# A decoder trunk on one core: round trips on SyncE's queue, polyphase matrices fetched a chunk ahead, products half a chunk later, the norm's sums added on GpSimd

## The chip, the cores and the metric

The kernel runs on one core of a Trainium2 chip. A core has five engines with queues of their own: TensorE (PE in the profile; PEld is its weight load), VectorE (DVE), ScalarE (ACT), GpSimd (POOL) and SyncE (SP), which here only issues transfers. Each engine works through its instructions in order and waits at its head for what the next one needs. The metric is the device time of one execution in microseconds.

## The reference

Two layers act on x of 512 tokens and 1024 features. Layer 0 has a causal Conformer convolution module, layer 1 differential attention; each is followed by a SwiGLU network and a gated per-layer embedding. The change lies in the convolution module:

```python
u = rms_norm(h, conv_norm_g[j])
a = x @ w_pw1 + b_pw1                                # here x is u
u = a[..., :D_MODEL] * jax.nn.sigmoid(a[..., D_MODEL:])
u = lax.conv_general_dilated(u, dw_w[:, None, :], window_strides=(1,),
    padding=[(CONV_WIDTH - 1, 0)], feature_group_count=D_MODEL) + dw_b   # 31 taps per feature
u = jax.nn.silu(layer_norm(u, ln_g, ln_b))           # mean and variance over 1024 features
return u @ w_pw2 + b_pw2
```

## The kernel before

Features lie on the 128 partitions, in 8 chunks of 128, and the 512 tokens along the free axis. Every product of the large matrices is made three times, with the operands split into a high and a low part (`mm3`). A weight tile comes from memory to `wraw` (2 buffers, SyncE's queue), ACT casts its high part to `whi`, DVE or GpSimd subtracts it to `wlo` (4 buffers each): `weight`, L137 to L150.

The convolution stage takes the chunks c = 0 to 7 in turn (loop at L407). Each has two halves of 24 matmuls, first for the gate, then for the value (`half`, L279). DVE and ACT form the gated product. The 31 taps of a chunk are then done one of two ways while the next chunk's halves run:

- Chunks 0, 1, 3, 5 and 7: some taps on TensorE with diagonal matrices (`pe_taps`: 4 for chunk 1, 14 for chunk 7), some on ACT and GpSimd (ACT multiplies, GpSimd adds, through four buffers `C2`/`C3`), the rest on DVE (`other_taps`).
- Chunks 2, 4 and 6 (`PHASED`): the product goes to memory and comes back with the tokens dealt to partitions by their remainder modulo 4 (`phased_in`: one store `pi`, four loads `C<-pi`). 36 products with 128 x 128 matrices do all taps (`phased_taps`). The result goes to memory and back the same way (`phased_out`: ACT copies it out of PSUM, store `po`, four loads `B<-po`, then one DVE operation).

Before the change, `phased_in` and `phased_out` issue their transfers on ACT's queue. The polyphase matrices come as twelve tiles a chunk with three matrices each, through six slots `D`, each issued just ahead of its three products.

The layer norm needs two sums over all features, of y and of its square. `moments` (L385) makes them on TensorE: for each chunk a product with a matrix of ones into `sums["mean"]` (L404; for chunks 1 to 7) and one into `sums["sq"]` (L405), fp32, 512 wide. After chunk 7, DVE takes the statistics (L454 to L459), a row is spread by L228, and y is shifted (L466 on DVE, L468 on GpSimd), scaled (L489), goes through SiLU (L490), is split (L492, L494) and enters the next matrix product. Products of the embedding's features (`project`) stand in TensorE's order there as fill.

The order on each engine is set by a scheduler that simulates the program; `tc.issue_after(x)` keeps what stands inside behind the instruction x. So the order of the source is only a wish.

Of the kernel before, what the change touches and what calls it, by code (L numbers as in the profile page):

```python
# [15 lines left out]
ALU = mybir.AluOpType  # L16
# [68 lines left out]
def trunk(ctx, tc, xT, pT, wts, diag, dww, vec, rel, onehot, lamv, out):  # L85
# [48 lines left out]

    wnext = [0]

    def weight(n=1024, pieces=1, between=(), eng=V):  # L137
        i = wnext[0]
        wnext[0] += 1
        raw = sb([P, 1024], "wraw", 2)  # L140
        hi = sb([P, 1024], "whi", 4, F32R)
        lo = sb([P, 1024], "wlo", 4, F32R)
        for k in range(pieces):
            cut = slice(k * n // pieces, (k + 1) * n // pieces)
            nc.sync.dma_start(raw[:, cut], wts[i, :, cut])
            if k < len(between):
                between[k]()
            A.copy(hi[:, cut], raw[:, cut])  # L148
            eng.tensor_tensor(lo[:, cut], raw[:, cut], f(hi[:, cut]), ALU.subtract)  # L149
        return hi, lo  # L150
# [86 lines left out]
    norm.chunk(0)  # L237
    w1 = weight(pieces=2, between=(load(1), load(2)))
    pairs = [(w1, w0)]
    for c in range(3, NC):  # L240
# [44 lines left out]
    def wt(c, j):  # L285
        return dwt[:, c * KW + j : c * KW + j + 1]

    def pe_taps(c):

# [5 lines left out]
        for j in range(PE_TAPS[c]):  # L295
            if j % 4 == 0:
                n = min(4, PE_TAPS[c] - j)
                dg = sb([P, 4, P], f"D{TAPS.index((c, j)) % 6}", 1)
                nc.sync.dma_start(dg[:, :n], diag[TAPS.index((c, j)), :, :n])
            last_tap[0] = T.matmul(  # L300
# [7 lines left out]
    def phased_in(c, src):  # L308

        d = dram.tile([P, S], F32, tag=f"pi{c}", name=f"pi{c}")  # L310
        nc.scalar.dma_start(d, src)
        xs = ups[c] = sb([P, NPH, LEAD + P], f"C{c // 2 % 2}", 2)
        G.memset(xs[:, :, :LEAD], 0.0)
        for i in range(NPH):
            nc.scalar.dma_start(
                xs[i * FG : (i + 1) * FG, :, LEAD:],
                bass.AP(d.tensor, d.offset + i * P, [[S, FG], [FG * S, NPH], [1, P]]),
            )

    def phased_taps(c, acc):  # L320
        for g in range(NPH):
            for m0 in range(0, LAGS, 3):
                i = TAPS.index((c, g, m0))
                dg = sb([P, 4, P], f"D{i % 6}", 1)
                nc.sync.dma_start(dg[:, :3], diag[i, :, :3])
                for m in range(m0, min(m0 + 3, LAGS)):
                    last_tap[0] = T.matmul(
                        acc[:, g * P : (g + 1) * P], dg[:, m - m0], ups[c][:, g, LEAD - m : LEAD - m + P],
                        start=(m == 0), stop=(m == LAGS - 1),
                    )  # L330

    def phased_out(c):
# [3 lines left out]
        d = dram.tile([P, S], F32, tag=f"po{c}", name=f"po{c}")  # L336
        nc.scalar.dma_start(d, o)
        both_ = sb([P, 2, S], f"B{c}", 1)
        for g in range(NPH):
            nc.scalar.dma_start(  # L340
                both_[g * FG : (g + 1) * FG, 1].rearrange("p (r n) -> p r n", r=NPH),
# [9 lines left out]
    def other_taps(c):  # L351
# [6 lines left out]
        for j in range(a, b):  # L358
            if j == a:
                A.activation(pacc, tap(j), AF.Identity, scale=wt(c, j), bias=col("dw_b", c))  # L360
            else:
                pr = sb([P, S], f"C{2 + j % 2}", 2)
                A.activation(pr, tap(j), AF.Copy, scale=wt(c, j))
                G.tensor_tensor(pacc, pacc, pr, ALU.add)
        yc = sb([P, S], f"B{c}", 1)
        alone = c in ALONE
# [14 lines left out]
    shrow = sb([P, S], "shrow", 1)  # L381
    sums = {}
    last_moment = [None]

    def moments(c):  # L385
# [8 lines left out]
        if c < SHIFT - 1:  # L394
            return
        for i in range(SHIFT) if c == SHIFT - 1 else (c,):
            if i == 0:
                sums["sq"] = tp()
            if i == 1:
                sums["mean"] = tp()  # L400
            sq = wk()
            A.activation(sq, y[i], AF.Square)
            if i > 0:
                T.matmul(sums["mean"], ones, y[i], start=(i == 1), stop=(i == NC - 1))  # L404
            last_moment[0] = T.matmul(sums["sq"], ones, sq, start=(i == 0), stop=(i == NC - 1))  # L405

    for c in range(NC):  # L407
# [6 lines left out]
        if c + 1 < NC:  # L414
            pairs.append((weight(), weight())[::-1])
        if c > 0:
# [28 lines left out]
    with tc.issue_after(last_tap[0].ins):  # L445
        moments(NC - 3)
        moments(NC - 2)
    moments(NC - 1)

# [453 lines left out]
def _layout(a):  # L903
# [44 lines left out]
    for i, (c, *at) in enumerate(TAPS):  # L948
        if c not in PHASED:
            for k in range(min(4, PE_TAPS[c] - at[0])):  # L950
                diag[i, np.arange(P), k, np.arange(P)] = dw[at[0] + k, c]
            continue
        g, m0 = at
        for m in range(m0, min(m0 + 3, LAGS)):
            for a_ in range(NPH):
                for b_ in range(NPH):
                    lag = NPH * m + b_ - a_
                    if 0 <= lag < KW:
                        diag[i, a_ * FG + f, m - m0, b_ * FG + f] = dw[KW - 1 - lag, c, g * FG + f]

# [40 lines left out]
```

## Time and profile before

| what | before |
|---|---|
| median of 3 runs | 1321.56 us (1321.38 to 1324.51) |
| profiled execution, whole time | 1322.03 us |
| its span, first to last instruction | 1320.2 us |
| matmuls on TensorE | 5852, mean clock 0.989 |
| convolution stage | 0 to about 192 us of the span |
| idle of TensorE in windows 0 to 26, 26 to 101, 101 to 192 us | 5.5, 0.6, 13.4 us |

In a timeline row stand the start in us, the time, engine and line, what is written from what, and in brackets the idle time before it and what ended it. One fp32 product is two rows on PE. A row of a group has its count behind x, then the busy time and the mean in ns, then idle time and its cause. A wait row has the sum in us, the count, and the longest. SPq and ACTq are the transfers that an engine's queue issues.

### The profile page before, as it was taken

How to read it: one execution, taken by the hardware profiler on the slowest of the kernel's cores; microseconds unless marked ns; L12 is line 12 of the kernel's file. 1: busy time of each engine (PE TensorE's matmuls, PEld its weight loads, DVE VectorE, ACT ScalarE, POOL GpSimd, SP SyncE). 2: the span in 40 equal slices, each digit the busy share in tenths (PEclk: the TensorE clock that was granted, in tenths of full speed). 3: DMA queues.
4: the chain of work that ended last, by engine and by line, in shares of the span. 5: the costliest groups of instructions: out<-in, count | busy, mean ns of one | idle time of the engine just before them, and what ended most of it. 6: DMA issues, size and time to landing. Idle time of an engine off the chain costs nothing. (4 is left out here: it accounts for less than half of the span.)

```text
span 1320.2 us, 15336 instructions
## 1 busy us (share of the span) xinstructions
PE 1283.0 (97%) x5852; PEld 1049.5 (79%) x5852; DVE 755.1 (57%) x1168; ACT 526.1 (40%) x830; POOL 258.4 (20%) x208
## 2 busy tenths in 40 slices
PE   8999889999999999999999998899999999999998
PEld 6777658888888888888888887778888888888887
DVE  6988684644344434455668887946543344334445
ACT  5644253422122222244466676734322222222342
POOL 5844342100000000022254544222000000000030
PEclk8999889999999999999999999999999999999999
DMA  6354412232322222233212321313223233332231
GB/s 218 110 170 155 132 33 94 82 97 98 104 98 98 97 96 96 80 104 102 87 65 83 102 73 41 103 34 126 96 96 96 96 97 99 102 97 93 76 123 65
DMA packets 45830, 129.21 MB, mean 98 GB/s; under 512 B 5267, under 2 KB 13587, under 8 KB 45756
## 3 DMA queue, kind: packets, MB, share of 16 engines
q1 hardware_dynamic: 39888, 122.70, 27.9%
q10 hardware_dynamic: 5868, 5.53, 1.3%
q8 instruction: 46, 0.75, 0.2%
q14 instruction: 28, 0.23, 0.1%
HBM read 124.52 MB, written 3.69 MB: 97 GB/s over the span
## 5 line engine op out<-in xcount | busy, mean ns | idle before, releaser
L148 ACT CAST whi<-wraw 128x1024 fp32r<-128x1024 f32 (+2 forms) x214 | 218.6, 1026 | 587.9 <-PE mm L156 367.8
L154 PE MATMUL mm<-A,wlo 128*128 128x512 f32 (+1 forms) x1096 | 426.0, 392 | 7.9 <-ACT A L492 3.8
L155 PE MATMUL mm<-A,whi 128*128 128x512 f32 (+1 forms) x1096 | 429.5, 393 | 1.4 <-DVE A L494 0.9
L156 PE MATMUL mm<-A,whi 128*128 128x512 f32 (+1 forms) x1096 | 426.9, 390 | 0.0
L149 DVE TENSOR_TENSOR wlo<-wraw,whi 128x1024 fp32r<-128x1024 f32 (+2 forms) x207 | 255.4, 1237 | 64.0 <-ACT whi L148 63.7
L154 PEld LDWEIGHTS mm<-A,wlo 128*128 128x128 f32 x1096 | 206.9, 189 | 54.7 <-ACT A L492 4.6
L155 PEld LDWEIGHTS mm<-A,whi 128*128 128x128 f32 x1096 | 207.0, 189 | 47.6 <-DVE A L169 3.2
L156 PEld LDWEIGHTS mm<-A,whi 128*128 128x128 f32 x1096 | 207.1, 189 | 43.5 <-issue 1.4
L188 POOL TENSOR_TENSOR acc<-acc,wk 128x512 f32<-128x512 f32 x42 | 68.6, 1632 | 781.8 <-issue 671.2
L155 PE MATMUL mm<-B,whi 128*128 128x512 f32 x352 | 136.9, 389 | 0.0
L156 PE MATMUL mm<-B,whi 128*128 128x512 f32 x352 | 136.9, 389 | 0.0
L154 PE MATMUL mm<-B,wlo 128*128 128x512 f32 x352 | 136.3, 389 | 0.0
L542 DVE TENSOR_TENSOR big<-mm,rb 128x512 f32<-128x512 f32 x44 | 30.4, 691 | 126.2 <-PE mm L156 126.2
L550 DVE TENSOR_TENSOR h<-mm,h 128x512 f32<-128x512 f32 x48 | 33.0, 691 | 120.7 <-PE mm L156 120.7
L540 DVE TENSOR_TENSOR big<-mm,rb 128x512 f32<-128x512 f32 x44 | 30.4, 691 | 99.3 <-PE mm L156 92.9
L154 PEld LDWEIGHTS mm<-B,wlo 128*128 128x128 f32 x352 | 66.1, 188 | 13.8
L156 PEld LDWEIGHTS mm<-B,whi 128*128 128x128 f32 x352 | 66.1, 188 | 13.7
L155 PEld LDWEIGHTS mm<-B,whi 128*128 128x128 f32 x352 | 66.1, 188 | 13.6
L156 PE MATMUL mm<-whi,A 128*128 128x512 f32 x192 | 75.7, 395 | 0.0
L155 PE MATMUL mm<-wlo,A 128*128 128x512 f32 x192 | 75.0, 396 | 0.0
L154 PE MATMUL mm<-whi,A 128*128 128x512 f32 x192 | 74.8, 396 | 0.0
L213 POOL TENSOR_TENSOR r<-v,mhalf 128x8 f32<-128x8 f32 (+1 forms) x31 | 47.5, 1532 | 121.7 <-DVE v L211 99.2
(193 smaller groups left out, 1426.1 us busy)
## 6 DMA issues: line engine op xcount, KB each, us to landing
wraw<-in_wts SPq DMA_DIRECT2D x194, 512.0 KB, 3.5
D<-in_diag SPq DMA_DIRECT2D x36, 192.0 KB, 3.9
wraw<-in_wts SPq DMA_DIRECT2D x16, 384.0 KB, 2.9
h<-in_xT SPq DMA_DIRECT2D x8, 256.0 KB, 5.3
bias<-scr ACTq DMA_DIRECT2D x8, 256.0 KB, 3.2
out_t<-h SPq DMA_DIRECT2D x7, 256.0 KB, 2.0
wraw<-in_wts SPq DMA_DIRECT2D x4, 256.0 KB, 3.4
wraw<-in_pT SPq DMA_DIRECT2D x4, 256.0 KB, 3.3
```

The source lines that it names most:

```text
L148: A.copy(hi[:, cut], raw[:, cut])
L149: eng.tensor_tensor(lo[:, cut], raw[:, cut], f(hi[:, cut]), ALU.subtract)
L154: T.matmul(acc, al, bh, start=first, stop=False)
L155: T.matmul(acc, ah, bl, start=False, stop=False)
L156: return T.matmul(acc, ah, bh, start=False, stop=last)
L188: self.eng.tensor_tensor(self.acc, self.acc, sq, ALU.add)
L213: last_pow[0] = G.tensor_tensor(r[:, :n], v[:, :n], mhalf[:, :n], ALU.pow)
L540: V.tensor_tensor(tg, pg, rb, ALU.mult)
L542: V.tensor_tensor(tu, pu, rb, ALU.mult)
L550: V.tensor_tensor(h[m], acc, h[m], ALU.add)
```

## The change

It has these parts, all in the convolution stage. The transfers of `phased_in` and `phased_out` are issued by SyncE, not ACT. The polyphase matrices come in tiles of four, nine tiles a chunk: for each of the four groups lags 0 to 3 and 4 to 7, and one tile with lag 8 of all groups; groups 2 and 3 use the `C5` buffers besides the `D` slots. All of a chunk's tiles are requested together, behind the weights of the chunk before (`after_weights`, with `pair_loads`). In the loop, the products of a phased chunk are written behind the next chunk's second half, not between its halves. The sums of the layer norm: the squares of chunks 1 to 6 are added on GpSimd to `sums["acc"]`, which starts as chunk 0's square, the values of chunks 1 to 6 to `macc`, and TensorE makes two products for each sum at the end. `issue_after(last_tap)` around `moments` is gone. An activation that calls for SiLU's table stands in chunk 7, ahead of its use.

```diff
-        TAPS += [(_c, g, m) for g in range(NPH) for m in range(0, LAGS, 3)]
+        TAPS += [(_c, g, m) for g in range(NPH) for m in (0, 4)] + [(_c, None, LAGS - 1)]
...
-            nc.sync.dma_start(raw[:, cut], wts[i, :, cut])
+            loaded[0] = nc.sync.dma_start(raw[:, cut], wts[i, :, cut])
...
+    def after_weights(c):
+        return tc.issue_after(pair_loads[c].ins)
...
     def phased_in(c, src):
-        nc.scalar.dma_start(d, src)
+        nc.sync.dma_start(d, src)
...
-            nc.scalar.dma_start(
+            nc.sync.dma_start(
                 xs[i * FG : (i + 1) * FG, :, LEAD:],
...
+    def phased_mats(c):
+        i = TAPS.index((c, 0, 0))
+        mats, k = [], 0
+        for g in range(NPH):
+            if g < 2:
+                two = []
+                for m in range(2):
+                    two.append(sb([P, 4, P], f"D{(i + k) % 6}", 1))
+                    nc.sync.dma_start(two[m], diag[i + 2 * g + m])
+                    k += 1
+            else:
+                both_ = sb([P, 2, 4, P], "C5", 2)
+                two = both_[:, 0], both_[:, 1]
+                for m in range(2):
+                    nc.sync.dma_start(two[m], diag[i + 2 * g + m])
+            mats.append(two)
+            if g == 0:
+                last = sb([P, 4, P], f"D{(i + k) % 6}", 1)
+                nc.sync.dma_start(last, diag[i + 2 * NPH])
+                k += 1
+        return mats, last
...
     def phased_taps(c, acc):
+        with after_weights(c):
+            mats, last = phased_mats(c)
         for g in range(NPH):
-            for m0 in range(0, LAGS, 3):
-                i = TAPS.index((c, g, m0))
-                dg = sb([P, 4, P], f"D{i % 6}", 1)
-                nc.sync.dma_start(dg[:, :3], diag[i, :, :3])
...
+            for m in range(LAGS):
+                w = last[:, g] if m == LAGS - 1 else mats[g][m // 4][:, m % 4]
...
         A.copy(o, accs[c])
-        nc.scalar.dma_start(d, o)
+        nc.sync.dma_start(d, o)
...
             if i == 0:
-                sums["sq"] = tp()
-            if i == 1:
-                sums["mean"] = tp()
+                A.activation(sums["acc"], y[0], AF.Square)
+                continue
             sq = wk()
             A.activation(sq, y[i], AF.Square)
-            if i > 0:
-                T.matmul(sums["mean"], ones, y[i], start=(i == 1), stop=(i == NC - 1))
-            last_moment[0] = T.matmul(sums["sq"], ones, sq, start=(i == 0), stop=(i == NC - 1))
+            if i < NC - 1:
+                G.tensor_tensor(sums["acc"], sums["acc"], sq, ALU.add)
+                if i > 1:
+                    G.tensor_tensor(macc, y[1] if i == 2 else macc, y[i], ALU.add)
+                continue
+            for n, part, one in (("mean", macc, y[i]), ("sq", sums["acc"], sq)):
+                T.matmul(sums[n], ones, part, start=True, stop=False)
+                last_moment[0] = T.matmul(sums[n], ones, one, start=False, stop=True)
...
             pg = half(wg)
-            pe_taps(c - 1)
+            if c - 1 not in PHASED:
+                pe_taps(c - 1)
             pa = half(wa)
+            if c - 1 in PHASED:
+                pe_taps(c - 1)
...
+        if c == NC - 1:
+            A.activation(sb([P, 8], "lam", 1), vt[:, :8], AF.Silu)
...
-            with tc.issue_after(last_tap[0].ins):
-                moments(c - 3)
+            moments(c - 3)
```

What the scheduler makes of it is seen at three places. The first is TensorE around chunk 6's products. Before, `mm_1129` takes chunk 6's products (L327, input `C_214`, matrices `D_230` and on), `mm_1104` is chunk 7's first half and `mm_1190` its second:

```order
L156 MATMUL mm_1104<-A_43_170,whi_967 128x512
L327 MATMUL mm_1129<-C_214_1040,D_230_1130 128x128 x3
L327 MATMUL mm_1129<-C_214_1040,D_231_1135 128x128 x3
L327 MATMUL mm_1129<-C_214_1040,D_232_1140 128x128 x3
L327 MATMUL mm_1129<-C_214_1040,D_233_1145 128x128 x3
L327 MATMUL mm_1129<-C_214_1040,D_234_1150 128x128 x3
L327 MATMUL mm_1129<-C_214_1040,D_235_1155 128x128 x3
L327 MATMUL mm_1129<-C_214_1040,D_236_1160 128x128 x3
L154 MATMUL mm_1190<-A_19_105,wlo_974 128x512
L327 MATMUL mm_1129<-C_214_1040,D_237_1165 128x128 x3
```

Now `mm_1134` takes them (L354), behind the last matmul of chunk 7's second half, which is `mm_1109`, and chunk 7's 14 taps (L306, `mm_1211`) follow at once:

```order
L157 MATMUL mm_1109<-A_43_170,whi_953 128x512
L354 MATMUL mm_1134<-C_202_1020,D_219_1135 128x128 x4
L354 MATMUL mm_1134<-C_202_1020,D_220_1137 128x128 x4
L354 MATMUL mm_1134<-C_202_1020,D_221_1139 128x128
L354 MATMUL mm_1134<-C_202_1020,D_222_1141 128x128 x4
L354 MATMUL mm_1134<-C_202_1020,D_223_1143 128x128 x4
L354 MATMUL mm_1134<-C_202_1020,D_221_1139 128x128
L354 MATMUL mm_1134<-C_202_1020,C_224_1145 128x128 x8
L354 MATMUL mm_1134<-C_202_1020,D_221_1139 128x128
L306 MATMUL mm_1211<-C_229_1194,D_234_1212 128x512 x4
```

The 36 products have moved from the front of chunk 7's second half to behind it. For chunks 2 and 4 the scheduler has put them inside the first or second half that follows, in one piece instead of two or three.

The second place is ACT at chunk 5's taps. Before, the copy of chunk 4's products (L335) and the transfers stand in ACT's order so (L363 are tap products, L422 a gate, L148 a cast):

```order
L335 COPY big_952<-sc_858 128x512
L363 ACTIVATE C_225_1075<-C_198_949,C_24_126 128x512
L337 DMA po_954<-big_952 128x512
L422 ACTIVATE big_1031<-big_1031,vec_63 128x512
L340 DMA B_200_956<-po_954 32x4x128 x4
L148 CAST whi_1380<-wraw_1379 128x1024
L402 ACTIVATE wk_1233<-B_200_956 128x512
L311 DMA pi_1038<-big_1036 128x512
L315 DMA C_214_1040<-pi_1038 32x4x128 x4
```

Now the copy (L362) stands behind eight of chunk 5's ten tap products (L390), and the squares (L434) go to GpSimd:

```order
L390 ACTIVATE C_209_1043<-C_186_929,C_24_126 128x512
L390 ACTIVATE C_210_1046<-C_186_929,C_24_126 128x512
L390 ACTIVATE C_211_1049<-C_186_929,C_24_126 128x512
L362 COPY big_932<-sc_871 128x512
L390 ACTIVATE C_212_1052<-C_186_929,C_24_126 128x512
L434 ACTIVATE wk_1080<-B_166_782 128x512
L390 ACTIVATE C_213_1055<-C_186_929,C_24_126 128x512
L149 CAST whi_1316<-wraw_1315 128x1024
```

No transfer of the round trips is left on ACT. The third place is SyncE, where they stand now: chunk 4's output (`po_934`, `B_188`) and chunk 6's input (`pi_1018`, `C_202`), with weights (L146) between them and the matrices of chunk 6 (L340) ahead:

```order
L340 DMA C_224_1145<-in_diag 128x512 x2
L340 DMA C_225_1148<-in_diag 128x512 x2
L305 DMA D_236_1224<-in_diag 128x512
L364 DMA po_934<-big_932 128x512
L367 DMA B_188_936<-po_934 32x4x128 x4
L146 DMA wraw_1450<-in_wts 128x1024
L317 DMA pi_1018<-big_1016 128x512
L146 DMA wraw_1456<-in_wts 128x1024
```

Two weight loads now stand behind a round trip that waits for ACT, DVE and a landing.

More of the change, by code (lines that the diff above doesn't have):

```diff
@@ L135, in trunk @@
     wnext = [0]
+    loaded = [None]
     def weight(n=1024, pieces=1, between=(), eng=V):
@@ L238, in trunk @@
     w1 = weight(pieces=2, between=(load(1), load(2)))
+    pair_loads = [loaded[0]]
     pairs = [(w1, w0)]
@@ L318, in phased_in @@
             )
+    def phased_mats(c):
[19 more added lines that the diff above has]
+        return mats, last
     def phased_taps(c, acc):
+        with after_weights(c):
+            mats, last = phased_mats(c)
         for g in range(NPH):
-            for m0 in range(0, LAGS, 3):
-                i = TAPS.index((c, g, m0))
-                dg = sb([P, 4, P], f"D{i % 6}", 1)
-                nc.sync.dma_start(dg[:, :3], diag[i, :, :3])
[L326 to L330, printed above, removed]
+            for m in range(LAGS):
+                w = last[:, g] if m == LAGS - 1 else mats[g][m // 4][:, m % 4]
+                last_tap[0] = T.matmul(
+                    acc[:, g * P : (g + 1) * P], w, ups[c][:, g, LEAD - m : LEAD - m + P],
+                    start=(m == 0), stop=(m == LAGS - 1),
+                )
     def phased_out(c):
@@ L364, in other_taps @@
                 G.tensor_tensor(pacc, pacc, pr, ALU.add)
-        yc = sb([P, S], f"B{c}", 1)
+        yc = sb([P, 2, S], f"B{c}", 1)
+        if c == 1:
+            sums["acc"] = yc[:, 1]
+        yc = yc[:, 0]
         alone = c in ALONE
@@ L382, in trunk @@
     sums = {}
+    macc = sb([P, S], "acc", 1)
     last_moment = [None]
@@ L396, in moments @@
         for i in range(SHIFT) if c == SHIFT - 1 else (c,):
+            if i == NC - 1:
+                sums["mean"], sums["sq"] = tp(), tp()
             if i == 0:
-                sums["sq"] = tp()
-            if i == 1:
-                sums["mean"] = tp()
+                A.activation(sums["acc"], y[0], AF.Square)
+                continue
             sq = wk()
             A.activation(sq, y[i], AF.Square)
-            if i > 0:
-                T.matmul(sums["mean"], ones, y[i], start=(i == 1), stop=(i == NC - 1))
-            last_moment[0] = T.matmul(sums["sq"], ones, sq, start=(i == 0), stop=(i == NC - 1))
+            if i < NC - 1:
[6 more added lines that the diff above has]
+                last_moment[0] = T.matmul(sums[n], ones, one, start=False, stop=True)
     for c in range(NC):
@@ L440, in trunk @@
         elif c > 3:
-            with tc.issue_after(last_tap[0].ins):
-                moments(c - 3)
+            moments(c - 3)
     pe_taps(NC - 1)
     other_taps(NC - 1)
[L445 to L448, printed above, removed]
+    for c in range(NC - 3, NC):
+        moments(c)
     vs = sb([P, P // 2], "v8", 2)[:, :8]
@@ L952, in _layout @@
             continue
-        g, m0 = at
-        for m in range(m0, min(m0 + 3, LAGS)):
+        g0, m0 = at
+        for k in range(4):
+            g, m = (k, m0) if g0 is None else (g0, m0 + k)
             for a_ in range(NPH):
```

7 lines of the change are left out of this document (4 added, 3 removed).

## The prediction

> **What bounds the kernel now.** I read the profile page first (busy times), then TensorE's waits up to 300 us, then busy times by stage. All three are quoted here; the stage rows begin with their stretch in us, and the last number but two is the granted clock.
>
> ```profile
> PE 1283.0 (97%) x5852; PEld 1049.5 (79%) x5852; DVE 755.1 (57%) x1168; ACT 526.1 (40%) x830; POOL 258.4 (20%) x208
> ...
> PE mm L327 <- DMA C<-pi: 5.8, 1, 5.8
> PE mm L154 <- ACT A L492: 3.8, 1, 3.8
> PE sc L327 <- DMA D<-in_diag: 2.9, 3, 1.5
> ...
> PE sc L731 <- DVE st L734: 5.7, 4, 1.7
> ...
> core 0: us, PE busy (x) PEld busy (x) DVE busy (x) ACT busy (x) POOL busy (x), PEclk, DMA share, GB/s
> 26.00:45.00 19.00, 19.00 (x78) 15.45 (x78) 14.65 (x18) 14.67 (x20) 8.19 (x6) 0.92 0.42 139
> ...
> 101.00:124.00 23.00, 20.35 (x119) 16.28 (x118) 20.07 (x25) 12.17 (x18) 13.78 (x11) 1.00 0.58 186
> 124.00:153.00 29.00, 23.20 (x126) 19.92 (x126) 15.35 (x20) 3.33 (x4) 2.48 (x3) 0.88 0.43 134
> 153.00:185.00 32.00, 32.00 (x98) 17.68 (x96) 25.33 (x38) 14.24 (x23) 17.73 (x11) 1.00 0.15 43
> 185.00:192.00 7.00, 2.08 (x6) 0.94 (x5) 7.00 (x7) 6.10 (x8) 6.94 (x5) 0.82 0.21 50
> ```
>
> TensorE is the bound: all its idle time is 1320.2 - 1283.0 = 37.2 us. So only two things can pay: work taken off TensorE, and waits of TensorE that go. The convolution stage, which the change rewrites, ends near 192 us. It loses 2.65 us between 101 and 124, 5.8 us between 124 and 153 (clock down to 0.88) and 4.9 us after 185. The wait rows name the causes: the re-laid input of chunk 6, the polyphase matrices, and the layer norm's last chain. The 5.7 us lie in the attention stage, far behind.
>
> **Part 1, the norm's sums.** Rows of TensorE's timeline, and its groups up to 300 us:
>
> ```profile
> 87.80 1.02 PE L405 MATMUL tp<-wk,ones 128*128 128x512 f32 x2
> 88.66 1.02 PE L404 MATMUL tp<-B,ones 128*128 128x512 f32 x2
> ...
> L405 PE MATMUL tp<-wk,ones 128*128 128x512 f32 x16 | 8.2, 592 | 0.0
> L404 PE MATMUL tp<-B,ones 128*128 128x512 f32 x14 | 7.2, 599 | 0.0
> ```
>
> One product is two rows; from one start to the next are 88.66 - 87.80 = 0.86 us. (16 + 14) / 2 = 15 products become 4, so 11 x 0.86 = **-9.5 us**. TensorE waits for nothing at these places (idle 0.0), so the time comes off its path. Bounds: -9.5, and -7.7 if the two of the eleven that lie after the last half are covered by the end chain (below). I take -9.5.
>
> **Part 2, matrices a chunk ahead.** 36 loads of 192 KB become 27 of 256 KB, queued ahead of the chunk that needs them. The three waits of 2.9 us go: **-2.9 us**. Bounds 0 (the slots wait as before) and -2.9; I take -2.9, since in the listed order a matrix's slot is freed two chunks before its next product.
>
> **Part 3, chunk 6's products half a chunk later.** TensorE's timeline, then DVE's and ACT's:
>
> ```profile
> 124.28 1.02 PE L404 MATMUL tp<-B,ones 128*128 128x512 f32 x2
> ...
> 129.67 0.39 PE L155 MATMUL mm<-A,whi 128*128 128x512 f32 x1
> ...
> 131.25 0.39 PE L156 MATMUL mm<-A,whi 128*128 128x512 f32 x1
> 137.44 6.95 PE L327 MATMUL mm<-C,D 128*128 128x128 f32 x42 [5.80 <-DMA C<-pi]
> ...
> 74.96 4.18 PE L327 MATMUL sc<-C,D 128*128 128x128 f32 x36
> ...
> 130.09 1.14 DVE L427 SCALAR_TENSOR_TENSOR big<-big,vec,big 128x512 f32<-128x512 f32 x1
> ...
> 131.27 0.34 ACTq L311 DMA_DIRECT2D pi<-big  x1
> 133.86 1.76 ACTq L315 DMA_DIRECT2D C<-pi  x4
> ```
>
> Chunk 6's second half ends at 124.28. Its input then goes through DVE (gate, to 131.23), out to memory and back in, and its products start at 137.44: 13.2 us. TensorE had one half to do meanwhile, 24 matmuls of (131.25 - 129.67) / 7 = 0.226 us, or 5.4 us, and two sums of 1.7 us: 13.2 - 7.1 = 6.1, the measured 5.8. Now both halves of chunk 7 lie between, 10.8 us, and the sums are gone: 13.2 - 10.8 = 2.4 us remain. The wait doesn't vanish, it shrinks.
>
> Whether 13.2 us holds is the unknown. Ahead of chunk 6's gate DVE still has chunk 4's output to finish, which comes the same way through memory:
>
> ```profile
> 118.61 0.34 ACTq L337 DMA_DIRECT2D po<-big  x1
> 122.58 1.76 ACTq L340 DMA_DIRECT2D B<-po  x4
> ...
> 125.98 1.15 DVE L345 SCALAR_TENSOR_TENSOR B<-B,vec,shrow 128x512 f32<-128x512 f32 x1 [2.46 <-DMA B<-po]
> ...
> 109.57 5.37 POOL L364 TENSOR_TENSOR wk<-wk,C 128x512 f32<-128x512 f32 x4 [9.56 <-ACT C L363]
> ...
> 157.00 9.83 POOL L364 TENSOR_TENSOR wk<-wk,C 128x512 f32<-128x512 f32 x6
> ```
>
> In the new order ACT copies chunk 4's products out behind eight of chunk 5's tap products, and ACT runs at most four of these ahead of GpSimd (four buffers). GpSimd now does three of the added sums before them. One addition takes 5.37 / 4 = 1.34 to 9.83 / 6 = 1.64 us, so the copy, and with it the gate, can come 3 x 1.5 = 4.5 us later. Bounds of the new wait: 0 (GpSimd was idle 9.56 us here, enough to cover it) and 2.4 + 4.5 = 6.9 us. I take 3.0, near the row. That is 3.0 - 5.8 = **-2.8 us**.
>
> The clock: 42 rows took 6.95 us where 36 take 4.18 with the full clock; 42 x 4.18 / 36 = 4.9, so the half clock after the wait cost 2.1 us. A wait of 2.17 us also brought it:
>
> ```profile
> 25.15 1.58 PE L228 MATMUL tp<-wk,ones 128*128 128x512 f32 x2 [2.17 <-DVE wk L218]
> ```
>
> That row lies just ahead of the stretch with clock 0.92. So I keep the loss: **0 us** of change (bounds -2.1 and +1). The Trainium skill (TensorE: Matmul & The Clock Gate, Part 1: The HAM clock gate) says that the rate halves after at least one idle window of about 3.4 us; by it a wait of 3.0 us should keep the full clock, and the sum would be 2.1 us lower. The 2.17 us row speaks against it, and I go by the row.
>
> **Part 4, the end chain.** TensorE, DVE, TensorE, ACT:
>
> ```profile
> 175.37 1.02 PE L405 MATMUL tp<-wk,ones 128*128 128x512 f32 x2
> ...
> 180.81 5.85 DVE L466 TENSOR_TENSOR B<-B,wk 128x512 f32<-128x512 f32 x3 [1.13 <-ACT wk L463]
> 186.58 1.87 DVE L489 TENSOR_TENSOR B<-B,tp 128x512 f32<-128x512 f32 x3
> ...
> 188.81 1.12 PE L154 MATMUL mm<-A,wlo 128*128 128x512 f32 x3 [3.81 <-ACT A L492]
> ...
> 185.73 1.28 ACT L490 ACT_TABLE_LOAD   x1
> ```
>
> From the last sum (175.37) to the next stage's first matmul (188.81) are 13.4 us, through statistics, DVE's three additions and SiLU. None of it changes, except that the means' four reductions can run before the squares' sum is there (8 reductions lie in 2 us, so up to -1), and SiLU's table, fetched earlier: 185.73 + 1.28 = 187.01 is hidden under DVE's 186.58 and its first operation, so nothing is gained; without that cover it is worth at most 1.3 us. Ahead of the last sum TensorE now has chunk 6's products, 72 x 0.116 = 8.4 us, the 14 taps and 20-odd fill matmuls, so chunk 7's y has time; but GpSimd starts chunk 7's taps only after ACT has copied chunk 6's products, and has to do three additions more. 9 x 1.6 us and the copy of 0.6 us, the last addition and square 1.4 us: 16.4 us, plus up to 1.5 us for chunk 6's y, against some 19 us of TensorE (14 taps and the shift 13, fill 5, two sums 1.7). It fits by about 1 to 2 us. **0 us**, bounds -1 and +3.
>
> **Part 5, transfers on SyncE's queue.** 30 issues of the round trips leave ACT, where casts stood behind them, and go to SyncE, ahead of weights. Weights have room:
>
> ```profile
> wraw<-in_wts SPq DMA_DIRECT2D x194, 512.0 KB, 3.5
> L148 ACT CAST whi<-wraw 128x1024 fp32r<-128x1024 f32 (+2 forms) x214 | 218.6, 1026 | 587.9 <-PE mm L156 367.8
> L149 DVE TENSOR_TENSOR wlo<-wraw,whi 128x1024 fp32r<-128x1024 f32 (+2 forms) x207 | 255.4, 1237 | 64.0 <-ACT whi L148 63.7
> ```
>
> A raw tile is free when the weight two before it is split, and that one's place when a half four before is done: a load runs some four halves ahead, 21.7 us, less 3.5 + 1.0 + 1.2 for landing, cast and split leaves 16 us. Per phased chunk SyncE waits about 4.0 us for the output to land (118.61 to 122.58), 2.6 for the input, and issues for 3.5: 10 us. Cover holds: **0 us**, bound +4.
>
> The 12 added sums on GpSimd can also hold DVE:
>
> ```profile
> 51.88 6.93 DVE L372 SCALAR_TENSOR_TENSOR sc<-C,C,sc 128x512 f32<-128x512 f32 x10
> ...
> 157.36 10.02 DVE L372 SCALAR_TENSOR_TENSOR B<-C,C,B 128x512 f32<-128x512 f32 x6
> ```
>
> Both ran beside a busy GpSimd: 0.69 us each with the accumulator in PSUM, 1.67 with everything in SBUF. So up to 12 x 0.98 = 11.8 us of DVE, bounds 0 and 11.8; DVE has 23 - 20.07 and 29 - 15.35 = 16.6 us idle between 101 and 153, and most of its work there is of the first kind. I take 0 on the path. The Trainium skill (SBUF — State Buffer, Who interferes with whom) states the rule: a VectorE instruction with two SBUF inputs contends with a GpSimd one that reads SBUF. The trace agrees, 1.67 against 0.69.
>
> **Sum.** The profiled execution took 1322.03 us around its span of 1320.2, 0.5 over the median of 1321.56. -9.5 - 2.9 - 2.8 = -15.2; 1322.0 - 15.2 = 1306.8, on the median's footing **1306.5 us**.
>
> **Rivals.**
> - The input of chunk 6 is there in time: no wait, full clock. 1306.5 - 3.0 - 2.1 = 1301.4. For it: GpSimd's idle 9.56 us, and no DMA waits on ACT. Against: 13.2 us are longer than 10.8.
> - GpSimd becomes the bound: the gate comes 4.5 us late (+3.9), and y of chunk 7 misses its 1 to 2 us (+3). 1306.5 + 6.9 = 1313.4. For it: 12 more additions of 1.3 to 1.6 us. Against: it is busy 20% of the span, and 2.48 of 29 us between 124 and 153.
> - The waits only move: DVE, not TensorE, sets the pace once TensorE has less to do, and the 9.5 and 2.9 us come back as waits for weights. About 1320. For it: 20.07 of 23 us busy between 101 and 124. Against: no wait for a split weight in those rows.
> - Slower: SyncE's order. Place: the weights queued behind chunk 4's output and chunk 6's input. Price: whatever the queue is held beyond 16 us, in each of three chunks. It turns slower than before by 4 us when each loses (15.2 + 4) / 3 = 6.4 us, that is when the queue is held 22 us instead of 10. That would be 1326 or more; I say 1328.
>
> **How the numbers follow.** Forecast 0.50, no wait 0.20, GpSimd 0.16, waits only move 0.08, slower 0.06. A measurement of this kernel can't tell less than 0.3%, 4 us, from no change. The first three lie below 1317.6: faster 0.86, same 0.08, slower 0.06. The range is 1299 to 1316: it takes in the first three cases, with 1 us of bound (the reductions) and change below the second and 2.6 us of part 5's bound above the third, and leaves out the last two and their edges, 0.2 in all.
>
> **What would show it.** Right: four rows of sums on TensorE in place of 15 products; no wait for the matrices; a wait of 2 to 4 us for C<-pi ahead of chunk 6's products, followed by clock 0.5; the end chain's wait as before. Wrong: waits of TensorE for wlo or whi before 130 us (SyncE or DVE the bound), a wait at the last sums for y or for the two GpSimd sums, or new waits in the attention part, whose order the scheduler has changed a little (the 5.7 us of waits there I leave as they are).

## The result, and the profile after

| | before | after |
|---|---|---|
| median of four runs, us | 1323.03 | 1313.01 |
| lowest to highest, us | 1321.38 to 1324.89 | 1311.65 to 1313.88 |
| profiled execution, us (span) | 1322.03 (1320.2) | 1313.88 (1312.1) |

The ratio is 0.9924, with a 95% interval from 0.9909 to 0.9939: 10.0 us faster, where 15.2 were forecast. (The time on record, 1306.5, is 6.5 below the median; 1.5 of that is the kernel before, whose median was 1321.56 in the earlier runs. 1321.56 - 15.2 is 1306.4; the 1306.5 is a slip of a tenth.) A second measurement of the same kernel, in the last group of experiments, gave 0.9921 (0.9908 to 0.9935).

The busy times of the changed kernel's engines:

```profile
PE 1276.4 (97%) x5830; PEld 1047.4 (80%) x5830; DVE 759.3 (58%) x1168; ACT 526.9 (40%) x832; POOL 276.1 (21%) x219
```

And TensorE's waits up to 300 us (us in total, times, longest):

```profile
PE mm L155 <- ACT A L533: 5.9, 1, 5.9
PE mm L354 <- DMA C<-pi: 5.5, 1, 5.5
...
PE sc L311 <- ACT big L362: 1.0, 1, 1.0
```

TensorE lost only 1283.0 - 1276.4 = 6.6 us of work, and the span 8.1. The wait for chunk 6's input (`C<-pi`) is as long as before, 5.5 against 5.8 us, and no wait for a matrix (`in_diag`) is left.

The convolution stage by stretches, in the columns of the rows before:

```profile
101.00:124.00 23.00, 22.01 (x126) 18.72 (x125) 19.24 (x22) 11.92 (x18) 22.35 (x17) 1.00 0.56 192
124.00:153.00 29.00, 23.47 (x114) 18.17 (x113) 26.50 (x28) 8.35 (x12) 17.49 (x13) 0.88 0.35 114
```

Between 124 and 153 TensorE has the same gap and the same clock of 0.88. What has changed there is DVE, 26.50 us busy of 29 after 15.35, and GpSimd, 17.49 after 2.48.

TensorE's timeline (start, duration, line, wait), with DVE's last operation on chunk 7's y (L405) and its first one behind the stage (L559), in the changed kernel; then the counterpart of L559 in the kernel before (L518):

```profile
134.87 6.94 PE L354 MATMUL mm<-C,D 128*128 128x128 f32 x36 [5.53 <-DMA C<-pi]
...
160.40 1.02 PE L441 MATMUL tp<-acc,ones 128*128 128x512 f32 x2
...
164.44 0.69 DVE L405 TENSOR_TENSOR B<-B,wk 128x512 f32<-128x512 f32 x1 [3.10 <-POOL wk L391]
...
166.44 1.02 PE L442 MATMUL tp<-wk,ones 128*128 128x512 f32 x2
...
180.08 2.13 PE L155 MATMUL mm<-A,wlo 128*128 128x512 f32 x4 [5.92 <-ACT A L533]
...
199.76 1.43 DVE L559 SCALAR_TENSOR_TENSOR h<-mm,vec,h 128x512 f32<-128x512 f32 x2 [9.41 <-PE mm L157]
```

```profile
209.65 1.43 DVE L518 SCALAR_TENSOR_TENSOR h<-mm,vec,h 128x512 f32<-128x512 f32 x2 [9.57 <-PE mm L156]
```

The last row is the first addition to `h` of the stage that follows. I use its start as a mark M: 209.65 - 199.76 = 9.9 us are gained ahead of it. Behind it these two executions take 1110.6 and 1112.3 us, so that the span gains only 8.1. The other mark is the start of chunk 6's products, which is the landing of their input: 137.44 before, 134.87 after. So the landing came 2.6 us earlier, and the way from it to M is 64.9 us long, not 72.2. The time divides there into two pieces with different causes. (L354 is 72 rows, two for each of the 36 products; the row above holds the first 36.)

What sets the landing? The changed kernel's DVE and its SyncE queue (SPq) around chunk 6's gate:

```profile
116.80 1.87 DVE L150 TENSOR_TENSOR wlo<-wraw,whi 128x1024 fp32r<-128x1024 f32 x1 [3.33 <-ACT whi L149]
118.59 1.54 DVE L402 SCALAR_TENSOR_TENSOR sc<-C,C,sc 128x512 f32<-128x512 f32 x2
120.03 2.03 DVE L372 SCALAR_TENSOR_TENSOR B<-B,vec,shrow 128x512 f32<-128x512 f32 x1
121.98 1.53 DVE L402 SCALAR_TENSOR_TENSOR sc<-C,C,sc 128x512 f32<-128x512 f32 x2
123.42 0.68 DVE L467 TENSOR_TENSOR big<-mm,rb 128x512 f32<-128x512 f32 x1
124.02 0.75 DVE L402 SCALAR_TENSOR_TENSOR sc<-C,C,sc 128x512 f32<-128x512 f32 x1
124.68 1.94 DVE L471 SCALAR_TENSOR_TENSOR big<-big,vec,big 128x512 f32<-128x512 f32 x1
...
126.64 0.34 SPq L317 DMA_DIRECT2D pi<-big  x1
...
128.76 0.33 SPq L146 DMA_DIRECT2D wraw<-in_wts  x1
129.19 1.81 SPq L321 DMA_DIRECT2D C<-pi  x4
```

Chunk 6's value half ended at 134.87 - 5.53 - 10.8 = 118.5 (two halves lie between). DVE then works without a gap through a weight split's end, taps of chunk 5 (L402) and chunk 4's output (L372) before it finishes the gate (L471) at 126.62. The store leaves at once, the loads 2.6 us later as before, and the last of them is issued at 131.00 and lands 3.9 us after that. From the half's end to the landing are 16.4 us, where the prediction had 13.2: 1.1 on DVE (8.1 against 131.23 - 124.28 = 7.0) and 2.1 behind the last issue (3.9 against 137.44 - 135.62 = 1.8).

### The profile page after: what moved, and what is told of

It reads as the page before. It is cut to its first block, busy times and chain, and to the rows that moved or that the text cites. A ratio compares the mean times of both kernels' runs of the same rounds, so it can differ in the third digit from the quotient of the medians.

```text
span 1312.1 us, 15285 instructions
## 1 busy us (share of the span) xinstructions
PE 1276.4 (97%) x5830; PEld 1047.4 (80%) x5830; DVE 759.3 (58%) x1168; ACT 526.9 (40%) x832; POOL 276.1 (21%) x219
## 5 line engine op out<-in xcount | busy, mean ns | idle before, releaser
L150 DVE TENSOR_TENSOR wlo<-wraw,whi 128x1024 fp32r<-128x1024 f32 (+2 forms) x207 | 257.5, 1248 | 66.6 <-ACT whi L149 66.2
```

## The experiments

The kernels of one heading ran on the same chip beside the kernel before; all give a ratio to it with its 95% interval. "Early" and "late" mean that the products of a phased chunk stand between the next chunk's halves, as before, or behind both, as in the change.

### First group: the parts by themselves

**Sums alone.** The kernel before, with only the norm's sums on GpSimd:

```diff
-            with tc.issue_after(last_tap[0].ins):
-                moments(c - 3)
+            moments(c - 3)          # and moments() as in the change
```

> The kernel before, with the sums' additions on GpSimd and nothing else of the change. Theory: 11 products x 0.86 us leave TensorE, and the wait for C<-pi, which had two sums (1.7 us) standing in it, grows from 5.8 to 7.5 us; the waits for D stay. 1323.0 - 9.5 + 1.7 = 1315 us. Rival 1: GpSimd's twelve added sums slow DVE and hold back chunk 6's gate, so the wait grows to 10 us or more: 1318 us or above. Rival 2: the additions are wholly hidden and the wait does not grow: 1313.5 us.

Ratio 0.9964 (0.9951 to 0.9977), 4.8 us. Transfers, DVE (chunk 6's gate, L437, and chunk 4's output, L345) and TensorE:

```profile
116.61 11.37 SPq L145 DMA_DIRECT2D wraw<-in_wts  x2
...
122.81 1.16 DVE L437 SCALAR_TENSOR_TENSOR big<-big,vec,big 128x512 f32<-128x512 f32 x1
...
125.35 1.14 DVE L345 SCALAR_TENSOR_TENSOR B<-B,vec,shrow 128x512 f32<-128x512 f32 x1 [0.80 <-DMA B<-po]
...
126.59 1.76 ACTq L315 DMA_DIRECT2D C<-pi  x4
132.33 6.27 PE L327 MATMUL mm<-C,D 128*128 128x128 f32 x36 [4.88 <-DMA C<-pi]
```

Only half of the 9.5 us came, about as much as the landing moved (5.1), and the wait shrank to 4.88 us, where theory and first rival had 7.5 and 10. The landing moved because the scheduler changed DVE's order too: chunk 6's gate stands ahead of chunk 4's output here and ends at 123.97, where before it stood behind that output and ended at 131.23. So this kernel doesn't test the sums by themselves. The loads were issued until 128.35 on ACT, with a weight on SyncE at 127.98, and landed 4.0 us later: the delay of the changed kernel is there with the two on different queues.

**Sums on TensorE.** The change, with its sums put back on TensorE:

```diff
-                G.tensor_tensor(sums["acc"], sums["acc"], sq, ALU.add)
+            if i > 0:
+                T.matmul(sums["mean"], ones, y[i], start=(i == 1), stop=(i == NC - 1))
+            last_moment[0] = T.matmul(sums["sq"], ones, sq, start=(i == 0), stop=(i == NC - 1))
```

> The changed kernel with the sums back on TensorE (15 products, no additions on GpSimd); all else as changed. Theory: 9.5 us come back, less what of them stands in the wait for C<-pi (5.5 us now): 1313.0 + 9.5 - 1.7 = 1321 us, and the wait is 3.5 to 4 us. Rival (the additions on GpSimd are what made the gate and the copy of chunk 4's products late): the copy of chunk 4's products comes some 4 us earlier, the 1.0 us wait for it is gone, the wait for C<-pi is 3 us or less: 1318 us.

Ratio 0.9933 (0.9918 to 0.9948), 8.9 us: nearly all of the gain without the part that was to bring most of it, and well below both the theory and its rival. TensorE, and DVE's last operation on chunk 7's y:

```profile
122.01 1.02 PE L435 MATMUL tp<-B,ones 128*128 128x512 f32 x2
...
135.45 4.26 PE L354 MATMUL mm<-C,D 128*128 128x128 f32 x36 [0.64 <-DMA C<-pi]
...
158.99 0.69 DVE L405 TENSOR_TENSOR B<-B,wk 128x512 f32<-128x512 f32 x1
...
165.64 1.02 PE L436 MATMUL tp<-wk,ones 128*128 128x512 f32 x2
...
179.09 2.13 PE L155 MATMUL mm<-A,wlo 128*128 128x512 f32 x4 [3.82 <-ACT A L530]
```

And its groups of sums from 134 to 190 us (two instructions make a product):

```profile
L435 PE MATMUL tp<-B,ones 128*128 128x512 f32 x8 | 4.2, 605 | 0.0
L436 PE MATMUL tp<-wk,ones 128*128 128x512 f32 x8 | 4.1, 592 | 0.0
```

The first of the timeline rows is the end of chunk 6's value half. By the groups, 8 of the 15 products lie behind the landing here, and the change has its 4 there. So of the 11 that it takes away, 7 lay ahead of the landing, 7 x 0.86 = 6.0 us, and the landing hardly notices (135.45 against 134.87). They come back as a wait: 0.64 becomes 5.53 us.

**Products early.** The change, with the products between the halves again:

```diff
             pg = half(wg)
-            if c - 1 not in PHASED:
-                pe_taps(c - 1)
+            pe_taps(c - 1)
             pa = half(wa)
-            if c - 1 in PHASED:
-                pe_taps(c - 1)
```

> The changed kernel with the products of a phased chunk written between the next chunk's halves, as before the change. Theory: C<-pi for chunk 6 lands at the same time (134.9 us of the span), but now only one half (5.4 us) stands ahead of the products, so the wait is 11 us in place of 5.5 and the time 5.4 us longer: 1318.5 us. Rival (the end of the stage is set by chunk 7's gate, its taps on DVE and GpSimd, not by TensorE): chunk 7's value half now ends later too, by 16 us, and the loss is 8 us or more: 1321 us or above. Rival 2 (a wait moves, nothing is lost): within 1.5 us of 1313.

Ratio 0.9973 (0.9963 to 0.9983), 3.6 us. TensorE:

```profile
133.86 6.71 PE L354 MATMUL mm<-C,D 128*128 128x128 f32 x36 [9.67 <-DMA C<-pi]
```

The landing is even 1.0 us earlier than in the change, and the kernel 6.4 us slower: behind the landing stands a half more.

**Round trips on ACT.** The change, with the transfers back on ACT's queue:

```diff
-            nc.sync.dma_start(
+            nc.scalar.dma_start(          # the store and loads of both phased_in and phased_out
```

> The changed kernel with the round trips' transfers back on ACT's queue. Theory (the order on SyncE's queue cost chunk 6's input 2 us, since a 512 KB weight goes just ahead of it): the four loads land 1.8 to 2 us after the last is issued, as before the change, not 3.9. But ACT issues them behind chunk 7's sigmoid (131.6 us in the changed kernel), so they are issued 2 to 3 us later: wait 5 to 6.5 us, time 1312.5 to 1314.5 us. Rival (the DMA engines are shared, whatever queue issues): landing stays 3.5 to 4 us after the last issue, wait 7.5 to 9 us, time 1315 to 1317 us.

Ratio 0.9940 (0.9925 to 0.9955), 7.9 us. The landing comes at 134.13, 2.5 us after the last issue, and M is 0.9 us ahead of the change's (198.85), less than two executions of the change differ (see the last group). The time behind M is longer by some 3 us (1115.2 against 1112.3), in the attention stage (L772, first to last row: 185.8 against 182.9), which the queue's change doesn't touch but whose order the scheduler makes anew. That SyncE's queue helps the convolution stage isn't shown.

### Second group: what holds the landing

**Weight behind the loads.** The 512 KB weight that stood just ahead of chunk 6's loads goes behind them:

```diff
+            with tc.issue_after(relaid[0].ins) if i == 19 else nullcontext():
                 loaded[0] = nc.sync.dma_start(raw[:, cut], wts[i, :, cut])
```

> The changed kernel with one exchange on SyncE's queue: the 512 KB weight that stands between chunk 6's store pi and its four loads C<-pi now stands behind them. Theory W (that weight is what makes the loads land 3.9 us after the last is issued, 1.8 before the change): loads issued 0.4 us earlier and landing in about 2 us, wait for C<-pi 3.0 to 3.5 in place of 5.5 us, 1311 us or less. Rival (DVE's order alone sets the landing, the transfer time differs for another reason): wait 5.0 to 5.5 us, time within 0.7 us of the changed kernel, 1312.5 to 1313.5 us.

Ratio 0.9928 (0.9909 to 0.9946), no gain on the change. SyncE, TensorE and DVE:

```profile
129.89 1.74 SPq L323 DMA_DIRECT2D C<-pi  x4
131.73 0.85 SPq L148 DMA_DIRECT2D wraw<-in_wts  x2
133.30 4.26 PE L356 MATMUL mm<-C,D 128*128 128x128 f32 x36 [1.15 <-DMA C<-pi]
...
143.31 0.74 DVE L481 SCALAR_TENSOR_TENSOR C<-big,vec,big 128x512 f32<-128x512 f32 x1
144.16 12.26 PE L308 MATMUL mm<-C,D 128*128 128x512 f32 x28 [2.58 <-issue]
```

The loads now land 133.30 - 131.63 = 1.7 us after the last issue, so here the weight is the cause of the 2 us. But the next row of TensorE, chunk 7's taps, then waits 2.58 us for chunk 7's gate, which DVE ends at 144.05. One wait has taken the other's place.

**Gate first.** Chunk 5's taps on DVE go behind chunk 6's gate:

```diff
+        with tc.issue_after(gate[6].ins) if c == 5 else nullcontext():
             for j in range(b, KW):
                 V.scalar_tensor_tensor(sum_, tap(j), wt(c, j), sum_, ALU.mult, ALU.add)
```

> The changed kernel with chunk 5's DVE taps held behind chunk 6's gate (five of them stand ahead of it in the changed kernel). Theory D (DVE's queue, not TensorE, sets when chunk 6's input leaves: five taps, slowed operations): the gate ends near 123.8 us of the span in place of 126.6; the loads then wait for the weight ahead of them, which waits for DVE's split, so they land near 132.5: wait 2.5 to 3.5 us, 1310 to 1311.5 us. Rival (the input is set by memory and queues, not by DVE): pi leaves earlier, the loads land at 134.9 as before, no gain, 1313 us.

Ratio 0.9914 (0.9889 to 0.9940), median 1310.52. DVE and TensorE:

```profile
121.69 1.37 DVE L473 SCALAR_TENSOR_TENSOR big<-big,vec,big 128x512 f32<-128x512 f32 x1
...
130.23 4.26 PE L355 MATMUL mm<-C,D 128*128 128x128 f32 x36 [0.80 <-DMA C<-pi]
...
139.34 0.75 DVE L481 SCALAR_TENSOR_TENSOR C<-big,vec,big 128x512 f32<-128x512 f32 x1
140.19 12.26 PE L307 MATMUL mm<-C,D 128*128 128x512 f32 x28 [1.68 <-POOL C L480]
...
148.76 10.13 DVE L404 SCALAR_TENSOR_TENSOR B<-C,C,B 128x512 f32<-128x512 f32 x6
```

The gate ends 3.6 us earlier (123.06), the landing comes 4.6 us earlier, and M 3.3 (196.47). The other 1.0 us lies behind the last issue (127.43): 2.8 us in place of 3.9, though a weight still stands just ahead of the loads. No work was taken away: it is the order on DVE that held most of the landing. By the median it is 2.5 us faster than the change, by the ratios 1.3, and the intervals overlap.

**Both gates first, and a copy ahead.** The next kernel also puts twelve taps of chunk 5 behind chunk 7's gate, the last operation of chunk 6 behind six taps of chunk 7, and has the weight behind the loads; the one after it adds ACT's copy of chunk 4's products ahead of four tap products:

```diff
+            rest[5] = lambda: (taps(b + 8, KW), close())     # run behind gate[7]
...
+                with tc.issue_after(copied[4].ins) if c == 5 and j >= a + 6 else nullcontext():
                     A.activation(pr, tap(j), AF.Copy, scale=wt(c, j))
```

> The changed kernel with chunk 5's DVE taps behind chunk 6's gate, 12 of them behind chunk 7's gate, chunk 6's last operation behind six of chunk 7's taps, and the weight behind the loads C<-pi. Theory D: loads land near 130 us, wait at most 1.3 us, the products run at the full clock and end near 138.5 in place of 145.7, chunk 7's taps follow at once: 1306 us. Rival (TensorE is no longer the bound; DVE and GpSimd have the same work as before and finish chunk 7's y and the last added sums at the old time): a new wait at the last sums, 1309.5 us or above.

> As the one before, and ACT's copy of chunk 4's products ahead of four of chunk 5's tap products. Theory: the wait of 1.0 us for that copy (chunk 5's shift product) goes as well, and chunk 4's y is there when DVE wants it: another 1 us, 1305 us. Rival (the copy delays the tap products and with them GpSimd, which is busy 22.35 of 23 us there): no change against the one before, or 1 us slower.

Both missed: 0.9922 (0.9908 to 0.9937) and 0.9913 (0.9899 to 0.9928), medians 1312.89 and 1311.36. DVE and TensorE of the first of the two:

```profile
129.30 4.18 PE L357 MATMUL mm<-C,D 128*128 128x128 f32 x36
...
137.69 0.75 DVE L507 SCALAR_TENSOR_TENSOR C<-big,vec,big 128x512 f32<-128x512 f32 x1 [6.18 <-PE mm L357]
...
163.40 1.18 PE L470 MATMUL tp<-B,ones 128*128 128x512 f32 x2 [2.18 <-DVE B L420]
```

The wait for chunk 6's input is gone, but chunk 7's gate now waits 6.18 us for the products of chunk 6 (it seems to take the place of their input; only the wait is shown), and a product of the last sums waits 2.18 us for a y on DVE. The copy ahead took away its wait of 1.0 us; the waits at the last sums stayed, and the 1.5 us between the medians lie within the intervals.

### Third group: the corner, and a mixture

**Sums on TensorE, products early.** Both edits above, so that only the matrices' loads, the queue and the early call for SiLU's table are left of the change:

```diff
+            pe_taps(c - 1)                 # between the halves
+            last_moment[0] = T.matmul(sums["sq"], ones, sq, start=(i == 0), stop=(i == NC - 1))
```

> The changed kernel with the sums back on TensorE and the products of a phased chunk back between the next chunk's halves: what is left of the change are the matrices fetched ahead and the transfers on SyncE's queue. It is the fourth corner of a square whose other three are measured as ratios to the kernel before: sums on GpSimd and products late (the change) 0.9924, sums on TensorE and products late 0.9933, sums on GpSimd and products early 0.9973. Theory (what counts is how much of TensorE's work stands behind the landing of chunk 6's input; work ahead of it is absorbed): moving the products alone is worth 7 to 9 us and the sums only what stands behind the landing, so this corner is 0.998 to 1.000, 1320.5 to 1323 us. Rival (each part takes its own work off the path and the parts add up): the sums' 9.5 us come on top of 1320, so 1327 us or above.

Ratio 0.9990 (0.9980 to 0.9999), 1.3 us, as the theory had it. TensorE:

```profile
134.64 6.50 PE L354 MATMUL mm<-C,D 128*128 128x128 f32 x36 [5.53 <-DMA C<-pi]
```

This closes a square, in us against the kernel before (ratio less one, times 1323):

| | sums on TensorE | sums on GpSimd |
|---|---|---|
| products early | -1.3 | -3.6 |
| products late | -8.9 | -10.0 |

Products later are worth 7.5 or 6.5 us, the sums 2.2 or 1.2 (the smaller figure lies within the intervals), what is left of the change 1.3. Along one way: -1.3 - 7.5 - 1.2 = -10.0.

**Mixture.** Gate first, weight behind, and the sums of the last chunks on TensorE again: those of chunks 5 to 7 (8 products), and in the second kernel of 4 to 7 (10 products):

```diff
-            if i < NC - 1:
+            if i <= 4:                     # 3 in the second
                 G.tensor_tensor(sums["acc"], sums["acc"], sq, ALU.add)
```

> Chunk 5's taps behind chunk 6's gate and the weight behind the loads C<-pi, as in the two runs with those edits; besides, chunks 5 and 6 are summed on TensorE (8 products at the end in place of 4, 3.4 us more on TensorE) and four additions leave GpSimd where they ran beside chunk 7's taps on DVE. Theory (behind the landing DVE and GpSimd, slowed by each other, set the end: chunk 7's y is ready at 160 us while TensorE has idle time): DVE's taps there fall from 1.69 to 1.3 us or less, the end comes 1 to 3 us earlier in spite of the added products: 1307.5 to 1310 us. Rival (TensorE is the bound again behind the landing): 3.4 us longer, 1313 us or more.

> As the one before with chunk 4's sums on TensorE too (10 products, 5.2 us more than in the changed kernel; six additions leave GpSimd, two of them beside chunk 6's gate). Theory: chunk 4's two products stand ahead of the landing of chunk 6's input and cost nothing there, the gate's operations on DVE are less slowed: within 1 us of the one before. Rival (TensorE bound): 1.7 us more than the one before.

Ratios 0.9902 (0.9887 to 0.9918) and 0.9904 (0.9886 to 0.9922), medians 1310.50 and 1310.69. DVE of the first:

```profile
150.31 6.53 DVE L406 SCALAR_TENSOR_TENSOR B<-C,C,B 128x512 f32<-128x512 f32 x6
```

Six taps of chunk 7 take 6.53 us, where "gate first" took 10.13 beside GpSimd's additions. But that brought the end no nearer: the last sum starts at 162.19 and M is 196.50, against 162.10 and 196.47 in "gate first", and the median is above the expected range. By their ratios these are the fastest kernels of the study; by the medians "gate first" (1310.52) is as fast, and the intervals of all three overlap with the change's. In the second mixture M is 1.8 us earlier still (194.73), which the median doesn't show.

### Fourth: the change once more

> The changed kernel once more, unaltered, beside the kernel before, to tell what in its trace repeats. Theory: the wait for C<-pi (5.5 us), the one for the copy of chunk 4's products (1.0) and the half clock after the wait repeat; the 1.7 us lost before 48 us do not, they are a later start and a longer stretch of half clock; 1312.5 to 1313.5 us, above both kernels with mixed sums (1310.5 and 1310.7). Rival: the wait varies with the start, 4 to 6.5 us, and the time reaches down to 1310.5.

The kernel is the change's, unaltered. Ratio 0.9921, median 1313.56. TensorE in this execution, and then in that of "gate first":

```profile
114.03 0.50 PE L311 MATMUL sc<-bias,ones 1*128 1x512 f32 x1 [1.26 <-ACT big L362]
...
115.03 0.63 PE L157 MATMUL mm<-A,whi 128*128 128x512 f32 x1
...
134.44 5.88 PE L354 MATMUL mm<-C,D 128*128 128x128 f32 x36 [3.13 <-DMA C<-pi]
```

```profile
113.77 0.49 PE L312 MATMUL sc<-bias,ones 1*128 1x512 f32 x1 [1.30 <-ACT big L363]
...
114.76 0.39 PE L157 MATMUL mm<-A,whi 128*128 128x512 f32 x1
```

The wait for chunk 6's input is 2.4 us shorter than in the first profile of the same kernel, and the landing only 0.4 us earlier: TensorE had been slowed by a half clock after the wait of 1.26 us (0.63 for a matmul of 0.39) and came later. What TensorE does ahead of the landing moves the wait, not the landing. M is 198.22 here, 1.5 us earlier than in the first profile, 1.1 of it behind the landing, where the first 36 rows took 5.88 us and not 6.94. So a difference of about 1 us in M between two single executions proves little.

## Why the prediction was right and wrong

The sign held, and 1313.0 lies in the range. That is partly luck: the sum was 5.2 us too large (15.2 for 10.0), and it wasn't further off because two wrong terms, the sums and the products, partly made up for each other. Of the signs that were to show it right, the four products and the missing waits for matrices came; the wait for chunk 6's input was 5.5 us (3.1 in the second execution), not 3.0, and the end chain's wait 5.9 us, not 3.8 as before. Each kernel's landing and its way to M, read as above:

| kernel | landing, us | landing to M, us | M, us | median less before's, us |
|---|---|---|---|---|
| before | 137.44 | 72.2 | 209.65 | |
| sums alone | 132.33 | 73.0 | 205.37 | -5.0 |
| sums on TensorE, products early | 134.64 | 72.8 | 207.44 | -1.3 |
| products early | 133.86 | 71.8 | 205.69 | -3.5 |
| sums on TensorE | 135.45 | 65.3 | 200.77 | -9.1 |
| the change | 134.87 | 64.9 | 199.76 | -10.0 |
| the change once more | 134.44 | 63.8 | 198.22 | -10.4 |
| round trips on ACT | 134.13 | 64.7 | 198.85 | -7.8 |
| weight behind | 133.30 | 65.7 | 198.99 | -10.1 |
| gate first | 130.23 | 66.2 | 196.47 | -12.4 |
| both gates | 129.30 (no wait) | 68.3 | 197.56 | -10.0 |
| both gates, copy ahead | 129.76 | 68.4 | 198.18 | -11.5 |
| mixture, 8 products | 130.11 | 66.4 | 196.50 | -12.5 |
| mixture, 10 products | 128.91 (no wait) | 65.8 | 194.73 | -12.3 |

Where there is no wait, the input had landed earlier than the figure says. The second column is some 72 with the products early and some 65 with them late; it is 68 in the two "both gates" kernels, where TensorE waits at the last sums instead. The first follows DVE's order and the transfers. M's differences agree with those of the medians to within about 1 us in all but three kernels.

**Part 1, -9.5 forecast, -1.2 to -2.2 measured inside the change.** The step that failed: "TensorE waits for nothing at these places (idle 0.0), so the time comes off its path." Idle 0.0 at an instruction says that it wasn't late, not that what follows can start sooner. Seven of the eleven products lay ahead of a landing that they don't set, so their 6.0 us became wait (0.64 to 5.53). Four lay behind it, 3.4 us, and they didn't bring the end nearer either: the last sum starts 31.6 us behind the landing in the change (30.5 in its second execution) and 30.2 with the sums on TensorE, and the next stage starts at 180.08 and 179.09. Two things went against it. The wait had brought the half clock, so that the first 36 rows of chunk 6's products took 6.94 instead of 4.26 us. And GpSimd, with the additions between its taps, held chunk 7's y: DVE's last operation on it waits 3.10 us for GpSimd and starts at 164.44, not at 158.99. TensorE had 23 matmuls of fill ahead of the last sum, not 14, so it didn't wait there; it waited later, 5.92 instead of 3.82 us. The 1.0 us of M (200.77 - 199.76) comes behind the next stage's start, where the slow matmuls (0.63 us) end 4.7 us after it and not 8.7. With the products early it is the same: the last sum starts 39.0 us behind the landing with the sums on GpSimd (172.84) and 38.1 with them on TensorE (172.76).

The rival "waits only move: DVE sets the pace" had the mechanism ahead of the landing, but priced it as if the whole change were lost, and named weights where the wait was for chunk 6's input. The rival "GpSimd becomes the bound" gave 1313.4, next to the median: its late y is in the trace, and the wait came nearer to its 6.9 us. Its price isn't confirmed: with the sums back on TensorE the kernel is no faster (0.9933 against 0.9924).

**Part 2, -2.9 forecast.** The matrices' waits are gone, as said. With the queue's change this moved the landing 2.8 us, M 2.2, and the median 1.3. The two were not tried apart on this kernel; with all else as in the change, the round trips on ACT landed 0.7 us earlier (134.13).

**Part 3, -2.8 forecast, -6.5 to -7.5 measured.** The step mis-sized: "the wait doesn't vanish, it shrinks", with 5.8 against 3.0 us as its price. That compared two waits as if the work around them stood still. A half of 5.4 us moved from behind the landing to ahead of it, where it is free; and with the sums still on TensorE the wait fell to 0.64 and the clock stayed full, 6.50 - 4.26 = 2.2 us more. 5.4 + 2.2 = 7.6, and the way to M shrank by 72.8 - 65.3 = 7.5. The lag itself was taken right where the sums stayed (135.45 - 122.01 = 13.4, forecast 13.2), and wrong with GpSimd's additions (16.4), though a weight stands ahead of the loads in both. The 4.5 us that ACT's copy might have cost did not come: DVE starts on chunk 4's output 1.5 us after the half's end (120.03, after 118.5), before it was 1.7 (125.98, after 124.28).

**Clock.** "I keep the loss" was right for the change (6.94 us for the first 36 rows). The Trainium skill (TensorE: Matmul & The Clock Gate, Part 1: The HAM clock gate) puts the step to half rate after at least one idle window of about 3.4 us, in windows that run free. By it the 3.13 us wait would have left the full clock; here 5.88 us instead of 4.26 followed, and even 1.26 us sufficed once, while 2.58 us ("weight behind") brought no half clock. The measurement decides.

**Part 4, 0 forecast.** From the last sum to the next stage are 180.08 - 166.44 = 13.6 us, before 13.4, so the chain itself is as long as forecast. But "it fits by about 1 to 2 us" failed: chunk 7's y waits 3.10 us for GpSimd, as told under part 1. SiLU's table wasn't fetched earlier either: the scheduler put the added call at 5.73 us, the sigmoid's table was loaded behind it at 32.54, and SiLU's again at 174.73, as at 185.73 before. That term of 0 says nothing of what an early table would bring.

**Part 5, 0 forecast.** The cover of the weights held: TensorE has no wait for a split weight up to 300 us. But a weight just ahead of chunk 6's loads held their landing: 3.9 us after the last issue in the change (3.1 in its second execution), 2.2 to 3.1 in four other kernels that have it there, 1.7 without it. Taking that away gained nothing, since chunk 7's gate on DVE came next. The Trainium skill (DMA: Bandwidth & Descriptors, Issuing engines are not separate DMA queues) says that transfers started by the scalar, sync or gpsimd engine run on the same 16 DMA engines and interleave, whichever engine started them. The trace agrees: 4.0 us with the two on different queues ("sums alone"), 3.9 on one, 1.7 without the weight.

**DVE beside GpSimd, 0 on the path forecast.** This was wrong: DVE is on the path, by chunk 6's gate. Here are all engines' busy times from 45 to 143 us, before and then after (the columns of the windows, as sums):

```profile
sum 98.00, PE 88.97 PEld 70.71 DVE 84.84 ACT 40.16 POOL 50.16; mean PE 22.24 PEld 17.68 DVE 21.21 ACT 10.04 POOL 12.54
```

```profile
sum 98.00, PE 91.23 PEld 76.55 DVE 92.11 ACT 42.29 POOL 65.82; mean PE 22.81 PEld 19.14 DVE 23.03 ACT 10.57 POOL 16.45
```

GpSimd does 15.66 us more, and DVE is busy 7.27 us longer, within the bounds given (0 to 11.8), and at 92.11 of 98 us busier than TensorE.

Open: the time behind M, where only the scheduler's order differs. It is 1110.6 us before, 1112.3 in the change, 1114.6 with both gates first and 1115.2 with the round trips on ACT, and the cause isn't known. In the second mixture it is 1112.9; its profiled execution (1309.36) was 1.3 us faster than its median, so the 2.6 us by which M runs ahead of the median are in part that.

## What to carry to other kernels

Before a saving on the busiest engine is counted, find the next wait behind it and ask who sets its end: work ahead of a landing that another engine's chain sets is worth nothing; the same work behind it can be worth all of its time, as the half was here, but only if nothing else holds the end, as GpSimd and the clock did for the four products. For a step that is moved across such a point, count the whole step, not the difference of the waits. Adding work to an idle engine is not free where its neighbour's queue holds the chain, and a look at the order of that queue (one gate behind five taps) can be worth more than the work removed.

## What was unexpected in the hardware

- Half clock came after waits of 1.26, 2.17, 3.13 and 5.53 us, and not after 0.99, 1.30, 1.68 and 2.58: no threshold can be read from these. The wait of 1.26 us cost more than itself: the eight matmuls from 115.03 to 118.43 took 3.4 us, where 8 x 0.227 = 1.8.
- Four small loads issued just behind or beside a 512 KB transfer landed 2.2 to 4.0 us after their last issue, and 1.7 to 1.8 us without it; the 4.0 had the large one on another queue.
- With GpSimd adding beside it, the same DVE operation took 1.94 instead of 1.14 us (chunk 6's gate), and a tap with all operands in SBUF 10.13 / 6 = 1.69 instead of 6.53 / 6 = 1.09, where GpSimd was busy for the first 2.8 us only.
